# A two-layer diffusion trunk on one core: experts taken chunk by chunk in pairs, the small work in steps, and modulation by row sums

## The chip, the cores and the metric

The kernel runs on one core of one Trainium2 chip. The metric is the device time of one execution in microseconds (us); the time before is the median of three runs. Five engines work side by side, each through its own instructions in a fixed order: TensorE (PE in the profile, its weight loads PEld), VectorE (DVE), ScalarE (ACT), GpSimd (POOL) and SyncE (SP), which here issues the DMAs. What an engine waits for are semaphores of the others.

## The reference, cut to what matters

Layer 0 is a bidirectional gated linear recurrence with a dense SwiGLU; layer 1 is windowed attention with a mixture of experts. Every sub-layer is modulated (shift, scale, gate) from a conditioning vector for the 256 latent tokens and from another for the 256 context tokens. Only latent tokens come out of layer 1.

```python
D_MODEL, SEQ, CTX_LEN, D_FF = 1024, 256, 256, 2816
N_EXPERTS, TOP_K, D_EXPERT = 8, 2, 3584
# modulation of a layer: silu(c) @ w_mod + b_mod  -> 6 parts of 1024 (shift, scale, gate, twice)
def moe_swiglu(h, router, w_gate_up, w_down):        # h: 256 latent tokens
    logits = h @ router
    gates = softmax of each token's two largest logits, zero for the other six experts
    for e in range(N_EXPERTS):
        g, u = split(h @ w_gate_up[e], 2)            # (1024, 7168)
        out += gates[:, e:e+1] * ((silu(g) * u) @ w_down[e])   # (3584, 1024)
```

## The kernel before, in words

All products run in fp32r. For accuracy each operand is split into a high part, the value rounded to fp32r by ScalarE (`hi = ACT copy`), and a low part, the rest (`lo = VectorE subtract`). `weights` loads 1 MB (128 x 2048 values) into a `raw` buffer by one DMA of SP's queue, makes `whi` on ScalarE and `wlo` on VectorE (`split_into`, lines 113 and 114). `mm3` is the product of two split operands in three matmuls: hi*hi, lo*hi, hi*lo (lines 129 to 131).

**Experts.** A kernel-made ranking puts the experts in the order 0 to 7 so that those with an even number ("heavy") have up to 128 tokens and those with an odd number ("light") up to 64. `gather` picks an expert's tokens with a one-hot matrix on TensorE (line 1196), applies shift and scale on ScalarE (1199) and splits the outcome (1202, 1203). A heavy expert's tokens are two stationary tiles (hi, lo) and take three matmuls a weight block; a light one's hi and lo stand side by side in the 128 columns of one tile, take two (1219, 1220), and the two halves are added by a matmul with `fold` (1262).

An expert has seven pieces of 512 hidden features. A piece needs six weights of 1 MB: four for gate and up (`moegu`, 48 matmuls of 512 columns when heavy, 32 when light) and two for down (`moed`, 24 or 16). `up` does the first four; the Silu and the product (1240 and 1242 for heavy, 1265 and 1269 for light) follow; `turned` transposes a heavy piece (1249), and `down` of a piece comes after `up` of the next one. When an expert ends, `finished` multiplies by the gate row and splits (1289), and `scatter` puts the rows back (1301 to 1303).

The loop `run` takes the experts one after another, 0 to 7: seven heavy pieces, seven light pieces, and so on. The small work of a stage (`later`) is emitted all at once at the next opportunity; the gather for experts 2 and 3 is emitted in one go after a weight of a light piece.

**Order.** A scheduler emits each engine's instructions by priority; `after(n)` hangs an instruction behind the split of the n-th weight that is prepared and not yet taken by TensorE. `take` keeps three weights prepared ahead. There are four `whi`, four `wlo` and, in this stage, nine `raw` buffers (four, four in the pool `late`, one in the place of `x`), so the DMA queue can run nine weights ahead of VectorE.

**PSUM.** The eight banks are four of tag `a` (gate and up, gather, scatter), two of `b` (down), two of `c` (transposes, fold).

**Modulation.** Two forms exist. `modulation` loads two 1 MB weights and multiplies on TensorE with 32-column stationary tiles (line 176), copies, transposes back (184) and reduces: it does all of layer 0 and chunks 10 and 11 of layer 1. Layer 0's chunks 10 and 11 are done between the two halves of the recurrence's out-projection, layer 1's two inside the attention loop (units 0 and 6). `modulation1` instead takes a transposed 1 MB weight and lets VectorE multiply each row with the conditioning row and sum it (line 221, four instructions a weight, two blocks of rows by two conditioning vectors): 20 such weights, one behind each hidden block of the dense SwiGLU.

Of the kernel before, what the change touches and what calls it, by code (L numbers as in the profile page):

```python
# [45 lines left out]
PE_MOD1 = (10, 11)  # L46
DVE_MOD1 = tuple(c for c in range(24) if c // 2 not in PE_MOD1)

# [6 lines left out]
class Trunk:  # L55
# [113 lines left out]
    def modulation(self, layer, cc, tag="a"):  # L169
# [3 lines left out]
        for kh in range(2):  # L173
            w = self.raw(self.ins["wmod0"][cc - 1, kh] if layer == 0 else self.ins["wmod1"][PE_MOD1.index(cc), kh], 2048).rearrange("p (k n) -> p k n", k=4)
            for j in range(4):
                nc.tensor.matmul(part[32 * j:32 * j + 32, :], self.cs[:, kh * 4 + j, :], w[:, j, :],
                                 start=(kh == 0), stop=(kh == 1), tile_position=(0, 32 * j))
# [3 lines left out]
        def finish():  # L181
# [3 lines left out]
            m = self.mod[layer][:, cc * 4:cc * 4 + 4, :]  # L185
            nc.vector.tensor_reduce(m, tr.rearrange("p (f j m) -> p f m j", f=4, j=4)[:, :, 0:2, :], axis=AX.X, op=ALU.add)
            self.modbias(layer, cc * 4, 4)
# [21 lines left out]
    def modbias(self, layer, f, n):  # L209
        m = self.mod[layer][:, f:f + n, :]  # L210
        b = self.bmod[:, layer, f:f + n].unsqueeze(2).to_broadcast([P, n, 2])
        self.nc.vector.tensor_tensor(m, m, b, op=ALU.add)

    def modulation1(self, n):

        nc = self.nc
        c = DVE_MOD1[n]
        w = self.raw(self.ins["wmod1t"][n], 2048).rearrange("p (b k) -> p b k", b=2)
        for b in range(2):
            for who in range(2):  # L220
                nc.vector.scalar_tensor_tensor(self.junk, w[:, b], 1.0, self.crow[:, who], op0=ALU.mult, op1=ALU.mult,  # L221
                                               accum_out=self.mod[1][:, 2 * c + b, who:who + 1])
        self.modbias(1, 2 * c, 2)
# [70 lines left out]
    def hgrn2(self):  # L294
        nc, ins = self.nc, self.ins
        with ExitStack() as es:
# [18 lines left out]
            def begin():  # L315

                with ExitStack() as es_st:
# [61 lines left out]
                    for d in range(KB):  # L379
                        now = [[t[:, at] for t in w] for at in cols(d)]  # L380
                        more = d == 0 or d % 2 == 1 and d < KB - 1
                        if more:
                            finish = self.modulation_block(1, "c") if d == 0 else self.modulation(0, (d + 1) // 2, "c")
# [190 lines left out]
            for hd in range(HEADS):  # L574
# [10 lines left out]
                if hd == HEADS - 1:  # L585
                    for i in range(HEADS - 2):
                        turn(i)
                    done += [self.modulation(0, c) for c in (8, 9)]
# [3 lines left out]
                done = [self.modulation(0, c) for c in {2: (4,), 4: (5,), 5: (6,), 6: (7,)}.get(hd, ())]  # L592
# [35 lines left out]
    def dense(self):  # L628
        nc, ins = self.nc, self.ins
        with ExitStack() as es:  # L630
            h = self.h
            for s in self.outproj(ins["hgout"], 0, (0, 1), [(d, 0) for d in range(4)] + [(0, 1)], HALF, self.squares):
                if s == 0:
                    late = [self.modulation(0, cc) for cc in (10, 11)]
                self.normalizer(s)
                self.modulated(0, 3, s)
            for f in late:
                f()
# [26 lines left out]

            def down(g, acts):
                for c in range(4):
                    w = [t.rearrange("p (k n) -> p k n", k=KB) for t in self.weights(ins["ffd"][g, c], 2048)]
# [48 lines left out]
            for f in range(2, FB):  # L717
# [3 lines left out]
                if f < 2 + len(DVE_MOD1):  # L721
                    self.modulation1(f - 2)
# [27 lines left out]
    def attention(self):  # L750
        nc, ins = self.nc, self.ins
        with ExitStack() as es:
# [162 lines left out]
            for n in range(len(units) + 3):  # L915
                if n in (4, 8):
                    normq(n // 4 + 1, queries(n // 4 + 1))
                if n in (0, 6):
                    finish = self.modulation(1, PE_MOD1[n // 6], "b")
# [4 lines left out]
                if n in (1, 7):  # L924
                    finish()
# [26 lines left out]
    def experts(self):  # L952
        nc, tc, ins = self.nc, self.tc, self.ins
        with ExitStack() as es:
# [12 lines left out]
            self.slots["raw"] += [(self.pool(es, "late"), 4), (None, 1)]  # L967
# [102 lines left out]
            def spare():  # L1070
                at = D + next(turns) % 2 * NT
                return rest[:, at:at + NT]

            def weigh():
# [4 lines left out]
                few, wide = spare(), spare()  # L1079
# [82 lines left out]
            ex = self.pool(es, "ex")  # L1162

# [10 lines left out]
            def gather(ks, over):  # L1174
# [3 lines left out]
                for k in ks:  # L1178
                    onehot(k, over, slice(at, at + P))
                    light = k % 2 == 1 and not over  # L1180
                    m = LIGHT if light else P
                    xe[k] = slice(at, at + m), self.h[k // 2 % 2][:, :, P:2 * P] if light else [t[:, :, k % 2 * P:k % 2 * P + P] for t in self.h]
                    at += P
# [6 lines left out]
                terms = [(src[:, i], hot[:, i, :width]) for src in (th, tl) for i in range(2)]  # L1190
                for c in range(4):
# [5 lines left out]
                    u = spare()[:, :2 * width].rearrange("p (k n) -> p k n", k=2)  # L1197
                    for q in range(2):
                        nc.scalar.activation(u[:, q], g[:, q], AF.Identity, scale=self.mcol(1, 4, 2 * c + q, 0), bias=self.mcol(1, 3, 2 * c + q, 0))
                    for cols, x in xe.values():  # L1200
                        hi, lo = [t[:, two] for t in x] if isinstance(x, list) else (x[:, two, :LIGHT], x[:, two, LIGHT:])
                        nc.scalar.activation(hi, u[:, :, cols], AF.Copy)
                        self.gathered = nc.vector.tensor_tensor(lo, u[:, :, cols], hi.bitcast(F32), op=ALU.subtract).ins
                out = {}
                for n, (k, (_, x)) in enumerate(xe.items()):
# [3 lines left out]
                    hotT = ex.tile([P, 2 * P], F32R, name="hotT", tag="hotT", bufs=3)  # L1209
                    nc.scalar.activation(hotT, tp[:, :2 * P], AF.Copy)  # L1210
                    out[k] = x, hotT
                return out
# [11 lines left out]
            def up(xe, ahead, later):  # L1224
                gu = [self.bank("a") for _ in range(2)]
                light = not isinstance(xe, list)
                out = [spare() for _ in range(1 + light)]
                for j in range(2):
                    for kh in range(2):
# [4 lines left out]
                        while later:  # L1234
                            later.pop(0)()
                    if light:
# [70 lines left out]
            def run(over, ready, early=()):  # L1307
# [47 lines left out]
                while later:  # L1355
                    later.pop(0)()
# [110 lines left out]
```

## Time and profile before

| | |
|---|---|
| median of three runs | 1922.15 us (1921.99 to 1923.66) |
| profiled execution | 1922.4 us, of which the span from first to last instruction is 1920.2 us |
| PE, PEld, DVE, ACT, POOL busy | 1840.5, 1515.9, 1517.8, 1098.6, 174.1 us |
| experts, from the first weight split to the end | about 967 to 1920 us of the span |
| read from HBM | 477.1 MB, 249 GB/s over the span |

A row of the profile names the source line, the engine, the operation and the tiles (out<-in). Matmuls overlap: the time from one start to the next, not the duration shown, is what a matmul costs in a full queue; the same holds to a smaller degree on VectorE.

### The profile page before, as it was taken

How to read it: one execution, taken by the hardware profiler on the slowest of the kernel's cores; microseconds unless marked ns; L12 is line 12 of the kernel's file. 1: busy time of each engine (PE TensorE's matmuls, PEld its weight loads, DVE VectorE, ACT ScalarE, POOL GpSimd, SP SyncE). 2: the span in 40 equal slices, each digit the busy share in tenths (PEclk: the TensorE clock that was granted, in tenths of full speed). 3: DMA queues.
4: the chain of work that ended last, by engine and by line, in shares of the span. 5: the costliest groups of instructions: out<-in, count | busy, mean ns of one | idle time of the engine just before them, and what ended most of it. 6: DMA issues, size and time to landing. Idle time of an engine off the chain costs nothing.

```text
span 1920.2 us, 29477 instructions
## 1 busy us (share of the span) xinstructions
PE 1840.5 (96%) x11516; PEld 1515.9 (79%) x11516; DVE 1517.8 (79%) x2033; ACT 1098.6 (57%) x1311; POOL 174.1 (9%) x168
## 2 busy tenths in 40 slices
PE   7999999999999999989999999999999999999997
PEld 5888887898888888877887877787687877878775
DVE  5787778578566664768488799988998889898897
ACT  3433333443222223457676789777886778867785
POOL 2243233100000000323300000000000000000000
PEclk8999999999999999999999999999999999999998
DMA  7312333366444442032569899999999999999994
GB/s 280 143 63 74 122 119 126 139 241 219 147 161 155 159 152 83 16 132 107 224 238 371 320 402 397 359 370 384 384 389 349 369 381 390 390 334 380 381 393 158
DMA packets 73810, 480.13 MB, mean 250 GB/s; under 512 B 8768, under 2 KB 11456, under 8 KB 18752
## 3 DMA queue, kind: packets, MB, share of 16 engines
q1 hardware_dynamic: 73664, 478.18, 65.5%
q8 instruction: 92, 1.51, 0.3%
q14 instruction: 54, 0.44, 0.1%
HBM read 477.10 MB, written 1.05 MB: 249 GB/s over the span
## 4 chain that ended last, share of the span: by engine, by line
PE 30%; DVE 13%; issue 6%; ACT 5%; DMA 0%; POOL 0%; DVEq 0%; ACTq 0%; POOLq 0%
DVE wlo L114 9%; PE ps_a L130 5%; PE ps_a L131 5%; PE ps_a L129 5%; ACT whi L113 4%; PE ps_b L129 2%; PE ps_b L130 2%; PE ps_b L131 2%; PE ps_a L1220 1%; PE ps_a L1219 1%; PE ps_b L1220 1%; PE ps_c L1262 1%; PE ps_b L1219 1%; PE ps_a L1196 1%; DVE acc L1303 1%
## 5 line engine op out<-in xcount | busy, mean ns | idle before, releaser
L114 DVE TENSOR_TENSOR wlo<-raw,whi 128x2048 fp32r<-128x2048 f32 (+2 forms) x382 | 798.6, 2118 | 63.7 <-ACT whi L113 63.4
L113 ACT ACTIVATE whi<-raw 128x2048 fp32r<-128x2048 f32 (+2 forms) x418 | 685.6, 1676 | 263.1 <-PE ps_a L130 207.9
L130 PE MATMUL ps_a<-hlo,whi 128*128 128x512 f32 (+1 forms) x800 | 283.4, 355 | 3.2 <-DVE hlo L286 3.0
L129 PE MATMUL ps_a<-hhi,whi 128*128 128x512 f32 (+1 forms) x800 | 283.2, 358 | 1.5 <-ACT hhi L113 0.7
L131 PE MATMUL ps_a<-hhi,wlo 128*128 128x512 f32 (+1 forms) x800 | 282.8, 354 | 0.2 <-POOL wlo L114 0.2
L130 PE MATMUL ps_a<-wlo,hhi 128*128 128x512 f32 (+1 forms) x720 | 257.2, 357 | 8.3 <-DVE wlo L114 8.3
L129 PE MATMUL ps_a<-whi,hhi 128*128 128x512 f32 (+1 forms) x720 | 258.5, 359 | 2.2 <-ACT hhi L361 2.0
L131 PE MATMUL ps_a<-whi,hlo 128*128 128x512 f32 (+1 forms) x720 | 255.5, 356 | 2.4 <-DVE hlo L363 2.4
L130 PEld LDWEIGHTS ps_a<-hlo,whi 128*128 128x128 f32 x800 | 152.4, 191 | 23.4 <-DVE hlo L286 4.0
L129 PEld LDWEIGHTS ps_a<-hhi,whi 128*128 128x128 f32 x800 | 151.5, 190 | 23.8 <-ACT hhi L113 1.1
L131 PEld LDWEIGHTS ps_a<-hhi,wlo 128*128 128x128 f32 x800 | 152.2, 191 | 20.4 <-POOL wlo L114 0.4
L130 PEld LDWEIGHTS ps_a<-wlo,hhi 128*128 128x128 f32 x720 | 138.2, 192 | 29.7 <-DVE wlo L114 11.0
L129 PEld LDWEIGHTS ps_a<-whi,hhi 128*128 128x128 f32 x720 | 138.4, 192 | 26.3 <-issue 2.8
L131 PEld LDWEIGHTS ps_a<-whi,hlo 128*128 128x128 f32 x720 | 138.0, 192 | 21.3 <-DVE hlo L363 2.9
L221 DVE SCALAR_TENSOR_TENSOR junk<-raw,crow 128x1024 f32<-128x1024 f32 x80 | 97.8, 1222 | 33.3 <-DMA raw<-wmod1t 32.0
L1220 PE MATMUL ps_a<-wlo,hlo 128*128 128x512 f32 x224 | 91.8, 411 | 10.2 <-DVE wlo L114 9.1
L1220 PE MATMUL ps_a<-wlo,hhi 128*128 128x512 f32 x224 | 91.7, 411 | 7.4 <-DVE wlo L114 6.7
L1219 PE MATMUL ps_a<-whi,hhi 128*128 128x512 f32 x224 | 90.7, 408 | 0.0
L1219 PE MATMUL ps_a<-whi,hlo 128*128 128x512 f32 x224 | 89.8, 404 | 0.0
L1220 PE MATMUL ps_b<-wlo,eahi 128*128 128x512 f32 x224 | 86.6, 416 | 3.1 <-DVE wlo L114 2.4
L114 DVE TENSOR_TENSOR wlo<-x,whi 128x2048 fp32r<-128x2048 f32 x37 | 84.6, 2287 | 4.1 <-ACT whi L113 4.1
L130 PE MATMUL ps_b<-wlo,eahi 128*128 128x512 f32 x224 | 87.8, 392 | 0.0
(382 smaller groups left out, 3067.5 us busy)
## 6 DMA issues: line engine op xcount, KB each, us to landing
raw<-moegu SPq DMA_DIRECT2D x185, 1024.0 KB, 7.4
raw<-moed SPq DMA_DIRECT2D x108, 1024.0 KB, 7.3
x<-moegu SPq DMA_DIRECT2D x37, 1024.0 KB, 7.6
raw<-wmod SPq DMA_DIRECT2D x26, 1024.0 KB, 5.5
raw<-ffgu SPq DMA_DIRECT2D x22, 1024.0 KB, 4.8
raw<-wmod1t SPq DMA_DIRECT2D x20, 1024.0 KB, 4.9
raw<-whead SPq DMA_DIRECT2D x14, 768.0 KB, 4.5
raw<-ffd SPq DMA_DIRECT2D x8, 1024.0 KB, 4.8
```

Of the source, the lines that this page charges most:

```text
L113: high = self.nc.scalar.activation(hi[:, at], x[:, at], AF.Copy)
L114: low = (by or self.nc.vector).tensor_tensor(lo[:, at], x[:, at], hi[:, at].bitcast(F32), op=ALU.subtract)
L129: mm(out, l[0], r[0], start=first, stop=False)
L130: mm(out, l[0], r[1], start=False, stop=False)
L131: mm(out, l[1], r[0], start=False, stop=last)
L221: nc.vector.scalar_tensor_tensor(self.junk, w[:, b], 1.0, self.crow[:, who], op0=ALU.mult, op1=ALU.mult, accum_out=self.mod[1][:, 2 * c + ...
L1196: nc.tensor.matmul(g[:, q], l[:, 2 * c + q], r, start=(n == 0), stop=(n == 3))
L1219: nc.tensor.matmul(out, l, r[0], start=first, stop=False)
L1220: nc.tensor.matmul(out, l, r[1], start=False, stop=last)
L1262: nc.tensor.matmul(to[:, f], x[:, f * P:(f + 1) * P], fold, start=True, stop=True)
L1303: nc.vector.scalar_tensor_tensor(acc[:, i, cols], o, gate[:, i, e:e + 1], acc[:, i, cols], op0=ALU.mult, op1=ALU.add)
```

## The change

Four edits go together.

1. **Pieces take turns.** `run` orders the work as two heavy pieces, then a heavy and a light piece by turns (heavy piece n beside light piece n-2), and at the end two light pieces. An expert pair (0 and 1, 2 and 3, ...) is therefore in work at the same time, so `b` has four banks, `a` three and `c` one.
2. **Small work in steps.** `gather`, `turned`, `folded` and `finish` become generators; `tick` runs one step of each after every weight, and each step's ScalarE and VectorE instructions are hung behind the split of a weight one to three ahead.
3. **Buffers.** The room for three scratch rows (`room`) and the light experts' tokens (`xl`) comes from the pool `late`: two `raw` buffers there in place of four, seven in all.
4. **Modulation.** Layer 0's chunks 10 and 11 (as blocks 20 to 23) and layer 1's chunks 10 and 11 go to VectorE's row sums, 28 weights in place of 20; layer 1's from block 8 on are summed for the latent vector alone. There are 80 row-sum instructions before and after. Eight of the 28 stand in the dense SwiGLU's two `down` calls.

```diff
-DVE_MOD1 = tuple(c for c in range(24) if c // 2 not in PE_MOD1)
+DVE_MOD = [(0, c, 2) for c in range(20, 24)] + [(1, c, 2 if c < 8 else 1) for c in range(24)]
...
-                if s == 0:
-                    late = [self.modulation(0, cc) for cc in (10, 11)]
...
             def down(g, acts):
                 for c in range(4):
+                    self.modulation_rows(next(rows))
...
-                if f < 2 + len(DVE_MOD1):
-                    self.modulation1(f - 2)
+                self.modulation_rows(next(rows))
...
-                if n in (0, 6):
-                    finish = self.modulation(1, PE_MOD1[n // 6], "b")
...
-            self.slots["raw"] += [(self.pool(es, "late"), 4), (None, 1)]
+            self.slots["raw"] += [(self.pool(es, "late"), 2), (None, 1)]
...
+            self.banks(a=3, b=4, c=1)
+            later = []
+            def tick():
+                for task in later[:]:
+                    if next(task, later) is later:
+                        later.remove(task)
...
                 for j in range(2):
                     for kh in range(2):
                         w = [t.rearrange("p (k n) -> p k n", k=4) for t in self.take(ahead)]
...
+                        if kh and light:
+                            with self.after(2):
+                                nc.scalar.copy(both[j], gu[j])
+                        elif kh and not j:
+                            later.append(turned(gu, act))
+                        tick()
...
+            def turned(gu, act):
+                yield
+                sg = spare(3)
+                with self.after(2):
+                    nc.scalar.activation(sg, gu[0], AF.Silu)
+                yield
+                yield
+                with self.after(1, True):
+                    self.mark = nc.vector.tensor_tensor(sg, gu[1], sg, op=ALU.mult).ins
+                yield
...
+                    heavy, light = ([(e, c) for e in range(i, NE, 2) for c in range(EC)] for i in range(2))
+                    work = heavy[:2]
+                    for n in range(2, len(heavy)):
+                        work += [heavy[n], light[n - 2]]
+                    work += light[-2:]
```

Two places in the built program show the move. The first is VectorE's order where a heavy expert ends (before: the first light piece has begun; the names: `x<-ps_b` is `finished`, `x<-ps_c` and `eahi<-x` the product and low part of a light piece).

```order
L114 TENSOR_TENSOR wlo<-raw,whi 128x2048 x5
L114 TENSOR_TENSOR wlo<-x,whi 128x2048
L1289 TENSOR_TENSOR x<-ps_b,x 128x512
L114 TENSOR_TENSOR wlo<-raw,whi 128x2048 x2
L1269 TENSOR_TENSOR x<-ps_c,x 128x256
L114 TENSOR_TENSOR wlo<-raw,whi 128x2048
L1273 TENSOR_TENSOR eahi<-x,eahi 128x4x64
L1289 TENSOR_TENSOR x<-ps_b,x 128x512
```

The same place of the changed kernel, where a light expert ends between two heavy pieces (`room<-ps_a` and `ealo<-ps_c` belong to a heavy piece, `room<-ps_b` is `finish`):

```order
L1270 TENSOR_TENSOR room<-ps_a,room 128x512
L113 TENSOR_TENSOR wlo<-raw,whi 128x2048 x2
L1322 TENSOR_TENSOR room<-ps_b,x 128x512 x2
L113 TENSOR_TENSOR wlo<-raw,whi 128x2048
L1282 TENSOR_TENSOR ealo<-ps_c,eahi 128x512
L113 TENSOR_TENSOR wlo<-raw,whi 128x2048
L1331 TENSOR_TENSOR ealo<-room,eahi 128x512 x2
L113 TENSOR_TENSOR wlo<-raw,whi 128x2048 x2
L1341 SCALAR_TENSOR_TENSOR acc<-ps_a,gate,acc 128x512
```

The multiplications by the gate row now stand together, and heavy and light steps lie between the same weight splits.

The second is ScalarE's order in the gather for a heavy and a light expert together (`mod_96` is the scale and shift; 192 columns are 128 heavy and 64 light tokens). Before:

```order
L1199 ACTIVATE x<-ps_a,mod_96 128x192 x2
L1202 ACTIVATE hhi<-x 128x2x128
L1202 ACTIVATE hhi<-x 128x2x64
L113 ACTIVATE whi<-raw 128x2048
L1199 ACTIVATE x<-ps_a,mod_96 128x192 x3
```

Changed:

```order
L1210 ACTIVATE room<-ps_a,mod_96 128x192 x2
L112 ACTIVATE whi<-raw 128x2048
L1214 ACTIVATE hhi<-room 128x2x128
L1214 ACTIVATE xl<-room 128x2x64
L1210 ACTIVATE room<-ps_a,mod_96 128x192 x2
L112 ACTIVATE whi<-raw 128x2048
L1214 ACTIVATE hhi<-room 128x2x128
L1214 ACTIVATE xl<-room 128x2x64
```

A weight split now lies in every step of the gather, and on TensorE eight weight matmuls or more lie between two of its steps.

More of the change, by code (lines that the diff above doesn't have):

```diff
@@ L167, in setup, with modulation @@
         self.mod = [c.tile([P, 48, 2], F32, name=f"mod{i}") for i in range(2)]
-    def modulation(self, layer, cc, tag="a"):
+    def modulation(self, cc, tag="a"):
         nc = self.nc
@@ L1172, in onehot, with gather @@
                 self.routed = made.ins
-            def gather(ks, over):
+            def gather(ks, over, ready):
                 at, xe = 0, {}
[L1178 to L1183, printed above, removed]
+                with self.after(1, True):
+                    for k in ks:
+                        onehot(k, over, slice(at, at + P))
+                        light = k % 2 == 1 and not over
+                        m, n = LIGHT if light else P, (k % 2 if over else k // 2 % 2) * P
+                        xe[k] = slice(at, at + m), xl[:, :, n:n + P] if light else [t[:, :, n:n + P] for t in self.h]
+                        at += P
                 if ks[0] == 0 and not over:
@@ L1222, in experts, with up @@
             block = lambda x, f: [t[:, f] for t in x] if isinstance(x, (list, tuple)) else x[:, f]
-            def up(xe, ahead, later):
+            def up(xe, ahead):
                 gu = [self.bank("a") for _ in range(2)]
                 light = not isinstance(xe, list)
-                out = [spare() for _ in range(1 + light)]
+                both, act = [spare(next(turns) % 3) for _ in range(2 * light)], []
                 for j in range(2):
@@ L1305, in scatter @@
                             nc.sync.dma_start(self.out[0, i * P:(i + 1) * P, cols], acc[:, i, cols])
-            def run(over, ready, early=()):
-                work = [(e, c) for e in range(NE) for c in range(EC)]
-                left, y, due, later = None, None, None, []
-                self.take, self.after = feed(work, early)
-                def finish(k, hotT, y):
-                    nonlocal due
-                    due = k, hotT, finished(y)
-                def prepare(*ks):
-                    ready.update(gather(ks, over))
+                        yield
@@ new lines, in run @@
+            def run(over, early=()):
+                if over:
+                    work = [(e, c) for e in range(NE) for c in range(EC)]
+                else:
+                    heavy, light = ([(e, c) for e in range(i, NE, 2) for c in range(EC)] for i in range(2))
[3 more added lines that the diff above has]
+                    work += light[-2:]
+                left, ready, at, ys = None, {}, {}, {}
+                self.take, self.after = feed(work, early)
+                later.append(gather((0,), over, ready))
+                drain()
@@ L1321, in run @@
                 for e, c in work + [(NE, 0)]:
[L1322 to L1323 removed]
                     if e < NE:
[L1325 to L1330 removed]
+                        if c == 0:
+                            at[e] = ready.pop(e)
@@ L1331, in run @@
+                        act = up(at[e][0], 0 if (e, c) == (0, 0) and early else 3)
+                    if e == NE or not left:
+                        drain()
                     if (e, c) == (0, 0) and not over:
```

208 lines of the change are left out of this document (103 added, 105 removed).

## Prediction

> **What bounds the kernel now.** I read the page's slices first, then busy times by stage, then VectorE's and TensorE's timelines inside one piece of each kind.
>
> ```profile
> PE   7999999999999999989999999999999999999997
> DVE  5787778578566664768488799988998889898897
> PEclk8999999999999999999999999999999999999998
> DMA  7312333366444442032569899999999999999994
> ...
> 430.00:710.00 280.00, 280.00 (x1293) 234.13 (x1292) 191.97 (x276) 70.81 (x62) 0.00 (x0) 1.00 0.47 166
> 1200.00:1321.00 121.00, 118.78 (x535) 97.05 (x535) 107.72 (x66) 85.62 (x61) 0.00 (x0) 1.00 0.97 366
> 1321.00:1437.00 116.00, 108.42 (x515) 85.99 (x514) 108.78 (x77) 98.27 (x92) 0.00 (x0) 0.97 0.99 388
> 1370.00:1415.00 45.00, 41.79 (x202) 33.66 (x201) 41.86 (x32) 39.29 (x46) 0.00 (x0) 0.92 1.01 423
> ```
>
> Each column is a slice of 48 us; the experts fill the right half. In the stretch rows the columns are TensorE, its weight loads, VectorE, ScalarE, GpSimd, granted clock, DMA share, GB/s. The dense layer (430 to 710) is TensorE alone. A heavy expert (1200 to 1321) is nearly so; in a light one (1321 to 1437) VectorE is as busy and TensorE idles and once loses its clock. No resource is far from full over the whole half, so the question is what each needs for a pair of pieces, and the timelines tell:
>
> ```profile
> 1245.24 2.29 DVE L114 TENSOR_TENSOR wlo<-raw,whi 128x2048 fp32r<-128x2048 f32 x1 [0.91 <-ACT whi L113]
> 1248.24 0.69 DVE L1242 TENSOR_TENSOR x<-ps_a,x 128x512 f32<-128x512 f32 x1 [0.71 <-PE ps_a L131]
> 1248.85 4.49 DVE L114 TENSOR_TENSOR wlo<-raw,whi 128x2048 fp32r<-128x2048 f32 x2
> 1253.85 4.48 DVE L114 TENSOR_TENSOR wlo<-raw,whi 128x2048 fp32r<-128x2048 f32 x2
> 1262.05 2.29 DVE L114 TENSOR_TENSOR wlo<-raw,whi 128x2048 fp32r<-128x2048 f32 x1 [1.51 <-ACT whi L113]
> 1265.06 0.69 DVE L1242 TENSOR_TENSOR x<-ps_a,x 128x512 f32<-128x512 f32 x1 [0.71 <-PE ps_a L131]
> ...
> 1374.77 0.42 DVE L1269 TENSOR_TENSOR x<-ps_c,x 128x256 f32<-128x256 f32 x1
> 1375.11 2.29 DVE L114 TENSOR_TENSOR wlo<-raw,whi 128x2048 fp32r<-128x2048 f32 x1
> 1389.06 0.42 DVE L1269 TENSOR_TENSOR x<-ps_c,x 128x256 f32<-128x256 f32 x1
> ...
> 1237.07 0.39 PE L129 MATMUL ps_a<-whi,hhi 128*128 128x512 f32 x1
> 1237.30 0.40 PE L130 MATMUL ps_a<-wlo,hhi 128*128 128x512 f32 x1
> 1384.11 1.00 PE L1262 MATMUL ps_c<-fold,x 128*128 128x64 f32 x8
> 1384.91 0.48 PE L1219 MATMUL ps_a<-whi,hlo 128*128 128x512 f32 x1
> ```
>
> A heavy piece recurs after 1265.06 - 1248.24 = 16.8 us, a light one after 1389.06 - 1374.77 = 14.3. A 512-column matmul starts every 0.23 us (0.227 when 48 are averaged), a low split every 4.48 - 2.29 = 2.2, an operation on 512 columns takes 0.6 (1248.24 to 1248.85), on 256 columns 0.34 (1374.77 to 1375.11). So a heavy piece is 72 x 0.227 + transposes 0.4 = 16.8 us of TensorE, gapless, with VectorE idle 2.2 of them (1.51 + 0.71). A light one is 48 x 0.227 + two fold groups of 0.8 = 12.5 us of TensorE but 6 x 2.2 + 2 x 0.34 = 13.9 of VectorE, and takes 14.3. The two kinds are bound by different engines, and each wastes the other's time.
>
> **Sum for an expert pair.** The same wait recurs where a light expert has begun:
>
> ```profile
> 1337.03 0.69 DVE L1289 TENSOR_TENSOR x<-ps_b,x 128x512 f32<-128x512 f32 x1 [2.67 <-PE ps_c L1262]
> 1572.50 0.69 DVE L1289 TENSOR_TENSOR x<-ps_b,x 128x512 f32<-128x512 f32 x1 [2.67 <-PE ps_c L1262]
> ...
> L1303 DVE SCALAR_TENSOR_TENSOR acc<-ps_a,gate,acc x32: 742/748/751, 1120.1 to 1912.7; 128x512 f32<-128x512 f32 x32
> ...
> 1168.55 0.39 PE L1196 MATMUL ps_a<-hot,hlo 128*128 128x192 f32 x2
> 1168.78 0.39 PE L1196 MATMUL ps_a<-hot,hhi 128*128 128x192 f32 x2
> ```
>
> Two experts take 235.5 us. By pieces that is 7 x (16.8 + 14.3) = 217.7; the other 17.8 are gather, scatter and the change of kind. Interleaved, each resource needs:
>
> - TensorE: 7 x (16.8 + 12.5) = 205.1, scatter 16 x 0.23 = 3.7, gather 32 matmuls, two in 0.23 us = 3.7, token transposes 0.5: 213.
> - VectorE: 84 x 2.2 = 184.8; heavy 7 x 2 x 0.6, light 7 x 2 x 0.34 = 13.2; two endings of 4 x 0.6 + 4 x 0.66 = 10; gather 3: 211.
> - DMA: 84 MB-loads of 1.049 MB = 88.1 MB at 423 GB/s = 208.
>
> TensorE stays last. The most that interleaving can give is 4 x (235.5 - 213) = 90 us.
>
> **What of it is lost.** A pair of pieces is 29.3 us on TensorE, 28.3 on VectorE, 12.58 MB / 423 = 29.7 on the DMA queue. Bounds for its true length: 29.3 (nobody waits) and 31.1 (nothing is evened out, 16.8 + 14.3). The weights' four `whi` slots even out little: over the six light weights TensorE needs 10.9 us and VectorE 13.2, a lag of 2.3, about the one split that stands ready. Each small step is hung behind the split of a weight one to three ahead; if its input is late, the next split queues behind it and TensorE waits for that weight. I take 0.4 over TensorE's 29.3, the DMA row being the nearest: 26 pairs, 10 us (ends 0 and 47).
>
> Gather: ScalarE does two activations, 0.50 each, and two copies of 0.41 and 0.30 in each step beside a 1.9 us split, 3.6 us against TensorE's 1.8 + 0.9. Four such steps put it up to 3.6 us behind; before, the same waits cost TensorE its clock:
>
> ```profile
> 1404.00:1408.00 4.00, 1.91 (x9) 1.91 (x10) 3.85 (x6) 3.15 (x6) 0.00 (x0) 0.73 1.01 420
> 1408.00:1413.00 5.00, 5.00 (x14) 3.89 (x14) 3.62 (x7) 4.41 (x8) 0.00 (x0) 0.53 1.02 423
> ...
> L1199 ACT ACTIVATE x<-ps_a,mod x40: 386/496/517, 961.7 to 1648.9; 128x192 f32<-128x192 f32 x24, 128x128 f32<-128x128 f32 x8, 128x64 f32<-128x64 f32 x8
> ...
>   PE ps_a L1196: 6.3, 3
> ...
> L1202 ACT ACTIVATE hhi<-x x24: 296/412/429, 962.5 to 1649.6; 128x256 fp32r<-128x256 f32 x16, 128x128 fp32r<-128x128 f32 x8
> ...
> L113 ACT ACTIVATE whi<-raw 128x2048 fp32r<-128x2048 f32 x291 | 545.4, 1911 | 30.9 <-PE ps_a L131 13.8 <-PE ps_b L131 7.0 <-issue 6.3
> ```
>
> TensorE waits 6.3 us for the activations in three waits and then runs at half clock (0.53). With eight weight matmuls between steps no such idle stretch is left. I take 2.5 us a gather, four of them: 10 (ends 0 and 14).
>
> Endings: 5 us of VectorE work each, of which 1 us a pair of pieces is covered by its slack; 0.75 each remains, eight: 6 (ends 0 and 40). The two light pieces left alone at the end stay at 14.3: 2 x 1.8 = 3.6. The start keeps its form: ranking, first gather and VectorE's waits there,
>
> ```profile
> 1021.63 6.70 DVE L114 TENSOR_TENSOR wlo<-raw,whi 128x2048 fp32r<-128x2048 f32 x3 [2.07 <-ACT whi L113]
> 1030.95 2.29 DVE L114 TENSOR_TENSOR wlo<-x,whi 128x2048 fp32r<-128x2048 f32 x1 [2.63 <-ACT whi L113]
> ```
>
> of which I leave 8 of the 90 (these two are 4.7; ends 0 and 12). Sum: 90 - 10 - 10 - 6 - 4 - 8 = 52.
>
> **Buffers.** Nine raw buffers become seven.
>
> ```profile
> raw<-moegu SPq DMA_DIRECT2D x185, 1024.0 KB, 7.4
> ```
>
> A load lands 7.4 us after its issue, three splits of 2.45; two buffers more are in ScalarE's and VectorE's hands. Five of seven would do. Cost 0, and its cover, the two left over, is 4.9 us; were it gone, see the first rival.
>
> The Trainium skill (DMA: Bandwidth & Descriptors, "Where 436 GB/s comes from") says that loads from HBM are bound by about 358 GB/s a core. By that a pair would take 35.1 us, more than 31.1, and the change would lose; the row above has 423 GB/s over 45 us, and the measurement decides.
>
> **Modulation.** Off the old paths come TensorE's chunks in the out-projection and in attention; to the dense layer goes VectorE work.
>
> ```profile
> L176 PE MATMUL ps_a<-raw,cs x32: 592/592/617, 394.6 to 397.7; 128*32 128x512 f32 x32
> L176 PE MATMUL ps_b<-raw,cs x32: 592/592/617, 831.3 to 869.0; 128*32 128x512 f32 x32
> ...
> L221 DVE SCALAR_TENSOR_TENSOR junk<-raw,crow x80: 1214/1224/1228, 429.3 to 704.9; 128x1024 f32<-128x1024 f32 x80
>   DMA raw<-wmod1t: 32.0, 10
> ...
> L291 DVE SCALAR_TENSOR_TENSOR x<-ps_a,mod,x x72: 473/483/491, 382.3 to 952.2; 128x256 f32<-128x256 f32 x72
> ```
>
> Two chunks hold TensorE from 394.6 to 397.7 and the last 0.6, about 3.6 us between the out-projection's halves; attention's two have the same 32 instructions, worth the same if TensorE sets the pace there and nothing if not. Ends 0 and 7, taken 5. In the dense layer the count of row sums is the same, 80; eight weights move into `down` steps, where VectorE then has 4 x 1.3 + 2.2 + 4 x 0.5 = 9.4 us under 48 x 0.227 = 10.9 of TensorE. The row sums wait for their own loads (32 us in ten waits), with the next weight's split queued behind them; TensorE was busy 280.00 of 280 in spite of it, and DMA runs at 166 GB/s there, so I cost it at 0 (to +8 if a `down` step loses its 1.5 us of cover).
>
> **Total.** The profiled execution took 1922.4 us (span 1920.2 and 2.2 around it; the median of the runs is 1922.15). 1922.4 - 52 - 5 = 1865.
>
> **Rivals.**
> - *The DMA queue becomes the bound* (slower). With two buffers fewer the rate falls to that of the heavy expert, 366 GB/s: a pair takes 34.4 us, 26 x 3.3 = +86, less some 25 for gathers, endings and modulation: 1983. It ends slower from about 393 GB/s down, where a pair's 32.0 us (12.58 MB) are 0.9 above the 31.1 now and eat the 25. Against it: 366 is just what a heavy piece asks for (6.29 MB / 16.8 = 375). The Trainium skill's rule above points this way.
> - *Turns do not even out* (the change does not do what it says): four `whi` slots are too few, ScalarE's copies of the small work stand behind a split each, and a pair stays near 31. Then only gathers, endings and modulation gain, 25 to 30: 1895.
> - *Nobody waits*: every pair 29.3, gathers and endings free: 90 - 4 - 8, and 7 for modulation: 1837.
>
> **Chances.** Forecast, 1850 to 1880: 0.56. Nobody waits: 0.14. No evening out, 1880 to 1915: 0.2. DMA bound: 0.05. The rest, about 1922, 0.05. So faster 0.93, same 0.02, slower 0.05; 0.2% is about what a measurement of this kernel can tell from no change. The range, 1838 to 1898, leaves out the DMA bound and the edges of two rivals.
>
> **What would show it.** Right: pieces of alternating kind with 29.3 to 30 us from one heavy product (line 1270) to the next; expert pairs of 216 to 222 us; DMA at 400 GB/s or more throughout; no half-clock stretch at a gather; TensorE still gapless in the dense layer, no line-176 rows there after 390 us. Wrong: VectorE or ScalarE waiting more than 1.5 us a pair (four slots), TensorE waiting for a bank `a` (three in place of four) whose copy stands behind a 1.9 us split, DMA at 370 with empty raw buffers, or a `down` step of the dense layer over 10.9 us.

## The result, and the profile after

The changed kernel takes 1861.25 us (1861.09 to 1863.59, four runs) against 1922.23 (1921.99 to 1923.66): a ratio of 0.9689, with a 95% interval of 0.967 to 0.9708. It is 61 us faster. The profiled execution took 1861.09 us, its span is 1859.3.

The slices of its page, 46 us each:

```profile
PE   8999999999999999998899999999999999999996
DVE  5787778679876453776748999999999999999997
PEclk8999999999999999999999999999999999999998
DMA  7412323426556452111338999999999999999994
```

TensorE, VectorE and the transfers are now all three at nine tenths or more through the experts; before, VectorE's digit went to and fro between 8 and 9. Stretches of the same kernel (columns as before: TensorE, weight loads, VectorE, ScalarE, GpSimd, clock, DMA share, GB/s):

```profile
430.00:710.00 280.00, 280.00 (x1280) 233.54 (x1279) 190.94 (x280) 71.43 (x63) 0.00 (x0) 1.00 0.55 199
1160.90:1378.80 217.90, 216.44 (x1033) 179.28 (x1033) 212.15 (x141) 182.62 (x149) 0.00 (x0) 1.00 1.00 405
1378.80:1596.80 218.00, 216.55 (x1034) 179.43 (x1033) 212.25 (x142) 182.72 (x149) 0.00 (x0) 1.00 1.00 405
1596.80:1809.10 212.30, 211.98 (x997) 175.42 (x997) 208.95 (x129) 176.78 (x131) 0.00 (x0) 1.00 1.01 412
```

The first is the dense layer, still gapless with the row sums in it. The others are three turns of two experts, bounded by the ending of a heavy one (line 1322); the clock stays at 1.00 in all three. VectorE's timeline shows the pairs of pieces inside the middle one (line 1297 is a light piece's product, once a pair):

```profile
1160.86 0.68 DVE L1322 TENSOR_TENSOR room<-ps_b,x 128x512 f32<-128x512 f32 x1
...
1378.82 0.68 DVE L1322 TENSOR_TENSOR room<-ps_b,x 128x512 f32<-128x512 f32 x1
...
1411.81 0.42 DVE L1297 TENSOR_TENSOR x<-ps_c,x 128x256 f32<-128x256 f32 x1
1440.10 0.42 DVE L1297 TENSOR_TENSOR room<-ps_c,room 128x256 f32<-128x256 f32 x1
1473.16 0.42 DVE L1297 TENSOR_TENSOR x<-ps_c,x 128x256 f32<-128x256 f32 x1
1502.76 0.42 DVE L1297 TENSOR_TENSOR x<-ps_c,x 128x256 f32<-128x256 f32 x1
1537.96 0.43 DVE L1297 TENSOR_TENSOR room<-ps_c,room 128x256 f32<-128x256 f32 x1 [0.45 <-ACT room L1294]
...
1596.76 0.68 DVE L1322 TENSOR_TENSOR room<-ps_b,x 128x512 f32<-128x512 f32 x1
```

Two experts take 218 us in place of 235.5. From one light product to the next the seven pairs take 33.3 (with an ending), 28.3, 33.1 (with the other ending), 29.6, 35.2 (with the gather), 28.8 and 29.7. The mark is an operation of VectorE, and a neighbour's weight split can fall on either side of it, so sums over several pairs say more than one pair.

Of TensorE's waits the one that shrank most is that for a light weight's low half. From the waits between 965 and 1860 us (what waited, for what: us in total, times, longest), first of the kernel before, then of the one after:

```profile
PEld ps_a L1220 <- DVE wlo L114: 36.9, 52, 1.9
```

```profile
PEld ps_a L1236 <- DVE wlo L113: 6.3, 16, 0.5
```

Ahead of the experts almost nothing is left of the gain. The last matmuls of the out-projection, the last mix of values in attention, and the first logit, before and after:

```profile
L130 PE MATMUL ps_a<-hlo,ohi x64: 280/283/283, 383.2 to 418.8; 128*128 128x256 f32 x64
...
L905 PE MATMUL ps_c<-pt,V x256: 272/273/477, 848.5 to 924.8; 128*64 128x128 f32 x128
...
L1039 DVE SCALAR_TENSOR_TENSOR logit<-ps_c,rstd,base x2: 216/220/225, 956.6 to 956.8; 128x8 f32<-128x8 f32 x2
```

```profile
L129 PE MATMUL ps_a<-hlo,ohi x64: 281/283/283, 383.3 to 415.4; 128*128 128x256 f32 x64
...
L902 PE MATMUL ps_c<-pt,V x256: 272/273/476, 840.3 to 925.0; 128*64 128x128 f32 x128
...
L1032 DVE SCALAR_TENSOR_TENSOR logit<-ps_c,rstd,base x2: 216/220/225, 955.6 to 955.8; 128x8 f32<-128x8 f32 x2
```

The out-projection ends 3.4 us earlier; attention ends where it did. From the logit to the end it is 1920.2 - 956.6 = 963.6 us before and 1859.3 - 955.6 = 903.7 after: 59.9 of the 61 us come from the experts.

### The profile page after: what moved, and what is told of

It is laid out like the page before. It is cut to its first block, busy times and chain, and to the rows that moved or that the text cites. A ratio compares the mean times of both kernels' runs of the same rounds, so it can differ in the third digit from the quotient of the medians.

```text
span 1859.3 us, 29342 instructions
## 1 busy us (share of the span) xinstructions
PE 1800.8 (97%) x11436; PEld 1504.2 (81%) x11436; DVE 1518.0 (82%) x2033; ACT 1101.6 (59%) x1307; POOL 175.2 (9%) x168
## 4 chain that ended last, share of the span: by engine, by line
PE 78%; DVE 11%; ACT 5%; issue 3%; DMA 1%; POOL 1%; SPq 0%; DVEq 0%; ACTq 0%; POOLq 0%
PE ps_a L128 16%; PE ps_a L129 16%; PE ps_a L130 16%; PE ps_a L1236 4%; DVE wlo L113 4%; PE ps_a L1235 4%; PE ps_b L129 3%; ACT whi L112 2%; PE ps_b L130 2%; PE ps_b L128 2%; PE ps_c L1291 2%; PE ps_b L1235 2%; PE ps_b L1236 2%; PE ps_b L461 1%; PE ps_c L538 1%
## 5 line engine op out<-in xcount | busy, mean ns | idle before, releaser
L112 ACT ACTIVATE whi<-raw 128x2048 fp32r<-128x2048 f32 (+2 forms) x404 | 670.1, 1681 | 290.5 <-PE ps_a L129 210.8
L113 DVE TENSOR_TENSOR wlo<-raw,whi 128x2048 fp32r<-128x2048 f32 (+2 forms) x368 | 772.7, 2127 | 39.0 <-ACT whi L112 38.1
L129 PE MATMUL ps_a<-wlo,hhi 128*128 128x512 f32 (+1 forms) x720 | 253.2, 352 | 0.8 <-DVE wlo L113 0.8
L1235 PE MATMUL ps_a<-whi,xl 128*128 128x512 f32 x448 | 178.7, 399 | 4.0 <-DVE acc L1341 3.7
L1236 PE MATMUL ps_a<-wlo,xl 128*128 128x512 f32 x448 | 177.9, 397 | 0.6
L113 DVE TENSOR_TENSOR wlo<-x,whi 128x2048 fp32r<-128x2048 f32 (+1 forms) x51 | 109.9, 2160 | 3.7 <-ACT whi L112 3.7
L1236 PEld LDWEIGHTS ps_a<-wlo,xl 128*128 128x128 f32 x448 | 84.8, 189 | 22.9 <-DVE wlo L113 6.3
L1235 PEld LDWEIGHTS ps_a<-whi,xl 128*128 128x128 f32 x448 | 84.8, 189 | 22.1 <-issue 5.6
L112 ACT ACTIVATE whi<-x 128x2048 fp32r<-128x2048 f32 (+1 forms) x51 | 92.3, 1815 | 15.7 <-PE ps_a L130 6.9
L129 PE MATMUL ps_b<-wlo,eahi 128*128 128x512 f32 x224 | 90.5, 404 | 2.3 <-DVE wlo L113 2.3
```

The costliest lines, as they stand in the source:

```text
L112: high = self.nc.scalar.activation(hi[:, at], x[:, at], AF.Copy)
L113: low = (by or self.nc.vector).tensor_tensor(lo[:, at], x[:, at], hi[:, at].bitcast(F32), op=ALU.subtract)
L129: mm(out, l[0], r[1], start=False, stop=False)
L1235: nc.tensor.matmul(out, l, r[0], start=first, stop=False)
L1236: nc.tensor.matmul(out, l, r[1], start=False, stop=last)
```

## The experiments

Twelve kernels in three sets, each set on one chip; the kernel before ran beside each set (1920.0, 1922.05 and 1922.5 us), so ratios to it are compared across sets.

**Modulation alone, and all but modulation.** One kernel is the old experts with the new rest, the other the new experts with the old rest. The edit between old and new rest, in short (the chunks' data and the other calls go with it):

```diff
-                if n in (0, 6):
-                    finish = self.modulation(1, PE_MOD1[n // 6], "b")
...
-                if f < 2 + len(DVE_MOD1):
-                    self.modulation1(f - 2)
+                self.modulation_rows(next(rows))
```

> The kernel before with the change's new modulation alone (twelve TensorE chunks become row sums in the dense layer and leave the out-projection and attention); experts untouched. The prediction's term is 5 us: 1917. Theory (gained and given back): the out-projection gains 3.4 us, attention, where the removed matmuls stood in idle time, gives most of it back: 1920 to 1922. Rival (a saving that stays): 1916 to 1918.

> The kernel after with the old modulation: TensorE's chunks stand again in the out-projection and in attention, the experts as changed. Theory (gained and given back): 1861 to 1863, nothing or 1 us above the changed kernel. Rival (a saving that stays): 1865 to 1867.

Measured: 1918.86 us (1908.52 to 1921.44), ratio 0.9993 (0.9982 to 1.0005), and 1863.96 us, ratio 0.9704 (0.969 to 0.9717), where the whole change has 0.9689 (0.967 to 0.9708) and its repeat below 0.97. Both medians lie between theory and rival. The new modulation is worth some 1 us by itself and 0 to 5 beside the new experts: the intervals hold no change, and do not exclude the 5. The traces above are sharper: gained and given back. It is the modulation's doing and not the new experts': the mix of values in attention runs from 841.4 to 924.6 us with the new modulation and the old experts, and from 850.1 to 926.5 with the old modulation and the new experts (before 848.5 to 924.8, after 840.3 to 925.0, above).

**Attention: who gave it back.** When the queries are normalized for the third time, the kernel after is still 4.3 us ahead (883.07 against 887.34 us); 40 us later it is not. With the modulation's weights gone from the stream, the raw buffers that they held let the out-projection's loads start earlier. From SP's timeline, before, then after:

```profile
868.79 21.32 SPq L105 DMA_DIRECT2D raw<-swout  x4
```

```profile
843.97 42.22 SPq L104 DMA_DIRECT2D raw<-swout  x4
```

So ScalarE splits five quarter weights in a row at 886.7 us, and GpSimd makes six low halves without a pause, in a stretch in which VectorE is the pace of attention. GpSimd before, then GpSimd and VectorE in the kernel after:

```profile
892.31 2.68 POOL L114 TENSOR_TENSOR wlo<-raw,whi 128x512 fp32r<-128x512 f32 x2 [4.91 <-ACT whi L113]
```

```profile
887.43 7.64 POOL L113 TENSOR_TENSOR wlo<-raw,whi 128x512 fp32r<-128x512 f32 x6 [4.02 <-ACT whi L112]
...
883.88 0.17 DVE L273 SCALAR_TENSOR_TENSOR rq<-rq 128x8 f32<-128x8 f32 x1
888.96 1.23 DVE L273 SCALAR_TENSOR_TENSOR rq<-rq 128x8 f32<-128x8 f32 x1
890.11 0.68 DVE L867 TENSOR_REDUCE st<-ps_a 128x1 f32<-128x512 f32 x1
893.86 1.23 DVE L870 TENSOR_TENSOR st<-st,rq 128x2 f32<-128x2 f32 x1
```

The same operation on 8 columns takes 0.17 us ahead of GpSimd's stretch and 1.23 in it, 1.06 us longer, where a low half takes 1.27; the reduction from PSUM keeps its 0.68. ScalarE then waits 2.95 us for VectorE (`st`, L871) and TensorE 3.18 for ScalarE, and a half-clock stretch of 6.8 us follows (granted clock 0.71 from 890 to 900, 1.00 in the kernel before). Three edits were run beside a repeat of the kernel after. `att_spread` hangs each quarter split of the out-projection behind a copy of turned scores:

```diff
+            self.held = self.pts[15:32]      # one copy of turned scores each
-            high = self.nc.scalar.activation(hi[:, at], x[:, at], AF.Copy)
+            with self.tc.issue_after(self.held.pop(0)) if self.held else nullcontext():
+                high = self.nc.scalar.activation(hi[:, at], x[:, at], AF.Copy)
```

`att_fill` puts unread products where the modulation's had been, and `att_both` does both:

```diff
+                if n in (0, 6):
+                    self.keep_warm(self.bank("b"), self.x[:, 1, 0], 4)
```

> The kernel after, unchanged, beside the next three on their chip: 1859 to 1863 by every theory; it is the base that they are measured against.

> The kernel after, but ScalarE's splits of the out-projection's first weights in attention are held so that at most one quarter weight is split behind each copy of turned scores, where the kernel after has five in a row at 884 to 888 us and GpSimd then six low halves in a row (887.4 to 895.1). Theory (GpSimd's low halves, which the freed raw buffers let come earlier and closer together, slow VectorE's small operations in the stretch where VectorE sets attention's pace, and so give back 4 of the 5 us that the modulation gained): VectorE's operations there return to 0.16 us and attention ends 3 to 4 us earlier, 1857 to 1858. Rival (the TensorE clock, or attention's own VectorE work, sets the end): no change, within 1.5 us of the base.

> The kernel after, with four matrix products whose result nobody reads (128x128 by 256 columns each, some 1.8 us together) put on TensorE at attention's units 0 and 6, where the kernel before had the modulation's matmuls. Theory (the removed matmuls had kept TensorE's clock up; without them a half-clock stretch of 6.8 us at 832 appeared): that stretch goes, and 2 to 4 us with it: 1857 to 1859. Rival (GpSimd's low halves against VectorE): no gain, 1861 to 1864.

> The kernel after with both edits of attention: ScalarE's quarter splits held to one a copy, and the four unread products at units 0 and 6. Theory (both edits gained by the same thing, that the run of five splits was broken up; the products did nothing for the clock): no better than either alone, 1857 to 1860. Rival (two separate causes, which add: 3.7 us and 5.6 us of attention): 1853 to 1855.

Measured: 1864.18 us (1862.96 to 1865.82) for the repeat, 1859.69 (1857.31 to 1862.76), 1857.91 (1856.93 to 1858.59) and 1857.89 (1856.64 to 1860.5). GpSimd and VectorE in `att_spread`, at the same place:

```profile
887.68 1.33 POOL L115 TENSOR_TENSOR wlo<-raw,whi 128x512 fp32r<-128x512 f32 x1 [4.02 <-ACT whi L114]
891.35 1.26 POOL L115 TENSOR_TENSOR wlo<-raw,whi 128x512 fp32r<-128x512 f32 x1 [2.34 <-ACT whi L114]
896.87 1.27 POOL L115 TENSOR_TENSOR wlo<-raw,whi 128x512 fp32r<-128x512 f32 x1 [4.26 <-ACT whi L114]
...
889.21 0.15 DVE L275 SCALAR_TENSOR_TENSOR rq<-rq 128x8 f32<-128x8 f32 x1
```

The low halves stand apart, the same small operation is at 0.15 us again (another, on 2 columns, still takes 1.26 beside the low half at 891.35), TensorE waits 1.62 us in place of 3.17 and keeps its clock (1.00 from 890 to 900, 0.86 in the repeat). Attention's last values are mixed at 921.5 us, in the repeat at 925.2: 3.7 us, as the theory named, but 0.9 of them were there at 884 us already, ahead of GpSimd's run, so 2.8 arise in it and behind it. The edit also takes ScalarE's five splits apart; in the repeat's trace it is VectorE that ScalarE and TensorE wait for there, so that is the likelier cause, though no run separates the two. `att_fill` was meant to test the clock. Its trace speaks against that: a half-clock stretch of 6.8 us stays at 837.8 (835.8 in the repeat), and up to 867 us it is within 1 us of the repeat. But GpSimd's low halves come two, one and three at a time as in the kernel before, the run of six is gone, and most of the 5.6 us (919.6) are gained behind 867. So it fits GpSimd's part without having been built for it, and how much of its gain the products themselves have stays open. Both together end attention at 917.4, earlier than either; the theory's "no better" holds for the total alone. In the profiled execution of `att_both` (1860.5 us, the longest of its five) longer half-clock stretches behind attention take it back: 10.2 us from 954.6 (6.8 in `att_fill`) and 3.4 us at each of two gathers (none in `att_fill`). By their ratios of 0.9667 and 0.9673, `att_fill` and `att_both` are the fastest kernels here that leave no product out, `att_fill` 6 us under the repeat.

The repeat itself is 3 us above the first measurement of the same kernel. Its trace has half-clock stretches of 3.4 us at two of the gathers (1102 and 1539 us), where the first trace has none, and the pairs there take 30.4 and 30.0 us in place of 28.8.

**The old order, with steps.**

```diff
-                if over:
+                if True:
                     work = [(e, c) for e in range(NE) for c in range(EC)]
```

and in the second also

```diff
-                    u = spare(4 - c % len(ks))[:, :2 * width].rearrange("p (k n) -> p k n", k=2)
+                    u = spare(c % len(ks))[:, :2 * width].rearrange("p (k n) -> p k n", k=2)
```

> The kernel after with the pieces in the old order (all eight of an expert, then all of the next), gathers, endings and the work of a piece still in steps. Theory (the turns carry the gain): light pieces are back at VectorE's 14 us and four expert pairs lose about 4 x 14 to 18 us: 1910 to 1925. Rival (the steps carry it, since they take the small work out of TensorE's way): 1865 to 1885.

> The same as the run with the pieces in the old order, with the gather's scratch moved to two tiles that are free in that order (there, the scratch of a gather and of a heavy piece were the same tile, which adds waits of one for the other). Theory (steps alone are worth 38 us, turns 21): 1880 to 1884, as before. Rival (the shared scratch had cost time): 1870 to 1878.

In the first of the two a gather's scratch and a heavy piece's product share a tile and overwrite one another, so its values are not the reference's; the second moves the scratch. They took 1881.95 us (ratio 0.9801, 0.9786 to 0.9817) and 1879.43 (0.978, 0.9765 to 0.9795). The theory that the turns carry the gain fell: all but the turns gains 42.6 us (steps, the gathers' new place, buffers, PSUM banks and modulation together), and turns another 15.3 (1879.43 to 1864.18, on one chip). The move of the scratch gained 2.5 us, or 4 by the ratios, and 1879.43 lies between its theory and its rival. Stretches of the second kernel, a light expert and then a heavy one, and the timeline of VectorE:

```profile
1340.00:1420.00 80.00, 76.49 (x364) 60.31 (x364) 80.00 (x49) 68.02 (x56) 0.00 (x0) 1.00 1.01 410
1210.00:1330.00 120.00, 120.00 (x567) 99.95 (x566) 111.11 (x77) 93.94 (x79) 0.00 (x0) 1.00 0.97 384
```

```profile
1330.01 0.68 DVE L1322 TENSOR_TENSOR room<-ps_b,x 128x512 f32<-128x512 f32 x1
1390.69 0.43 DVE L1297 TENSOR_TENSOR x<-ps_c,x 128x256 f32<-128x256 f32 x1
1404.57 0.43 DVE L1297 TENSOR_TENSOR x<-ps_c,x 128x256 f32<-128x256 f32 x1
1552.21 0.68 DVE L1322 TENSOR_TENSOR room<-ps_b,x 128x512 f32<-128x512 f32 x1
```

In the light expert VectorE is busy 80.00 of 80 us, and a piece takes 13.9 (14.3 before); in the heavy one TensorE is busy 120.00 of 120. Each kind is at its own bound without turns, and a turn of two experts takes 222.2 us. The gathers also moved: before, they stood in light pieces, where VectorE has no time (1389.06, 1404.37 and 1423.94 on its timeline of before: 15.3 and 19.6 us for two pieces of 14.3); now they stand behind a heavy expert's fifth piece.

**Gathers in one go, endings in two goes**, both with turns:

```diff
-                        later.append(gather((e + 1,) if over else (e + 2, e + 3), over, ready))
+                        for _ in gather((e + 1,) if over else (e + 2, e + 3), over, ready):
+                            pass
```

```diff
             def finish(e, hotT, y):
...
-                with self.after(1, True):
-                    for n in range(2):
-                        nc.vector.tensor_tensor(yg[n], y[n], gf[:, n * NT:(n + 1) * NT], op=ALU.mult)
-                yield
...
+                for n in range(2):
+                    nc.vector.tensor_tensor(yg[n], y[n], gf[:, n * NT:(n + 1) * NT], op=ALU.mult)
+                    self.split_into(hi, lo, yg[n])
+                for _ in range(3):
+                    yield
...
-                        yield
-                        with self.after(1, True):
-                            nc.vector.scalar_tensor_tensor(acc[:, i, cols], o, gate[:, i, e:e + 1], acc[:, i, cols], op0=ALU.mult, op1=ALU.add)
+                        nc.vector.scalar_tensor_tensor(acc[:, i, cols], o, gate[:, i, e:e + 1], acc[:, i, cols], op0=ALU.mult, op1=ALU.add)
```

> The kernel after with the three gathers of two experts each run in one go, as before the change, where the change gives them a step a weight; everything else as changed. Theory (a gather in one go makes TensorE wait for its activations and drops the clock): half-clock stretches of 3 to 7 us at each gather come back, 3 x 3 to 6 us: 1869 to 1880. Rival (with pieces taking turns TensorE has work enough to cover a gather, or the queue behind catches up): 1860 to 1863.

> The kernel after with each expert's ending in two goes, as before the change (scaling and split at once, then all scatter products and accumulations of four tiles at once three weights later), where the kernel after has nine steps, each placed behind a weight's split. The prediction's term for endings was 1 us each, about 8 in all, of which 6 would stay. Theory (steps took VectorE's bursts out of the weights' way, and most of the 32 us that steps gained beside the three gathers' 10.5 come from here): 1873 to 1885. Rival (an ending is covered by a pair's slack of 1 us of VectorE and by the buffers): 1861 to 1867.

Measured: 1871.73 us, ratio 0.9749 (0.9735 to 0.9764), and 1878.1, ratio 0.9782 (0.9759 to 0.9804). Against the change's 0.9689 and 0.97 in two sets these are 9 to 12 us for three gathers and 16 to 18 for eight endings. The pair with the gather, and the clock at another:

```profile
1509.91 0.41 DVE L1297 TENSOR_TENSOR x<-ps_c,x 128x256 f32<-128x256 f32 x1
1548.56 0.42 DVE L1297 TENSOR_TENSOR room<-ps_c,room 128x256 f32<-128x256 f32 x1
```

```profile
1529.00:1534.00 5.00, 4.69 (x16) 3.48 (x17) 2.04 (x7) 4.21 (x11) 0.00 (x0) 0.66 0.98 406
```

It is 38.7 us against 35.2, here with a stretch of half clock. The other two gathers in one go have none and still take 38.5 and 37.8 us against 35.9 and 35.2: the total lies in the theory's range, but the clock that it named is the smaller part, and what makes up the rest was not isolated. Of the endings in two goes the waits between 1130 and 1830 us tell, where the kernel after had 6.3 us in 16:

```profile
PEld ps_a L1236 <- DVE wlo L113: 23.3, 30, 2.1
```

The next weight's low half stands behind an ending's burst on VectorE, and TensorE waits for it. So gathers and endings in steps hold 25 to 30 of the 43 us that all but the turns gained, if they are worth as much without turns, which was not run.

**Five raw buffers.**

```diff
-            self.slots["raw"] += [(self.pool(es, "late"), 2), (None, 1)]
+            self.slots["raw"] += [(None, 1)]
```

> The kernel after with five raw weight buffers in the experts instead of seven. The prediction held that five would do and costed the step from nine to seven at 0. Theory (a load lands in some 7.9 us, three splits of 2.4; two more buffers are in the hands of ScalarE and VectorE): 1861 to 1866. Rival (transfers need more of them in flight to reach 430 GB/s): a pair of pieces over 31 us, 1905 or more.

Measured: 1879.45 us, ratio 0.9789 (0.9762 to 0.9816). Neither theory: 17 to 19 us slower than with seven, by the ratios of two sets. Waits between 1130 and 1830 us, and a turn of two experts:

```profile
ACT whi L112 <- DMA raw<-moegu: 44.0, 69, 2.1
...
ACT whi L112 <- DMA x<-moegu: 13.4, 22, 2.0
...
ACT whi L112 <- DMA raw<-moed: 8.1, 14, 0.8
...
ACT whi L112 <- DMA x<-moed: 3.0, 5, 1.0
```

```profile
1388.60:1612.00 223.40, 218.47 (x1033) 180.55 (x1032) 213.53 (x141) 185.37 (x149) 0.00 (x0) 0.99 0.99 395
```

With seven, no wait for a transfer stands in the list of the same stretch; with five ScalarE waits 68.5 us in 110 places, plain pairs of this turn are at 29.7 to 30.8 us, and the rate falls to 395 GB/s.

**What bounds a pair next.**

```diff
-                    self.mm3(out, l, r, first, last)
+                    nc.tensor.matmul(out, l[0], r[0], start=first, stop=False)
+                    nc.tensor.matmul(out, l[0], r[1], start=False, stop=last)
```

> The kernel after with two products in place of three for each block of a heavy expert's pieces (the low half of the activations times the high half of the weights is left out), so that TensorE's work in a pair of pieces falls from 29.3 to about 23.9 us. It asks what bounds a pair next. The prediction's bounds were 28.3 us for VectorE and 29.7 for the transfers at 423 GB/s. Theory (VectorE is next): pairs of 28.3, 26 us less, 1836 to 1842, at 445 GB/s. Rival (the transfers bound at 423 to 432 GB/s): pairs of 29.1 to 29.7, 1858 to 1864, no gain.

Measured: 1849.24 us, ratio 0.9628 (0.9602 to 0.9654): half of what the theory expected. A turn of two experts, its four pairs around the two endings and its three with the gather, then the same four and three in the kernel after:

```profile
1373.10:1589.70 216.60, 196.25 (x865) 146.04 (x866) 211.33 (x141) 180.86 (x148) 0.00 (x0) 0.98 1.00 408
1372.80:1496.00 123.20, 110.72 (x481) 80.83 (x480) 123.20 (x82) 101.26 (x76) 0.00 (x0) 1.00 1.01 414
1496.00:1589.40 93.40, 85.54 (x385) 65.19 (x384) 88.13 (x62) 79.60 (x72) 0.00 (x0) 0.96 0.98 399
```

```profile
1378.50:1502.80 124.30, 123.98 (x580) 101.92 (x579) 123.45 (x82) 102.55 (x77) 0.00 (x0) 1.00 1.00 407
1502.80:1596.50 93.70, 92.57 (x455) 77.50 (x455) 88.80 (x62) 80.17 (x72) 0.00 (x0) 1.00 0.99 403
```

A turn takes 216.6 us, only 1.4 less, although TensorE has 7 x 24 x 0.227 = 38 us less to do in it. The four pairs around the endings are VectorE's: busy 123.20 of 123.20 us here, and 123.45 of 124.3 in the kernel after. The three with the gather keep their length for another reason. Neither engine is full there: TensorE waits 3.2 us for ScalarE's copy of the token transposes (`hotT`) and then has a half-clock stretch of 6.8 us, which the trace of the kernel after does not have. Whose those three pairs are in the kernel after, this run cannot tell. The third turn has no gather, and there it can: its last three pairs take 88.1 us in the kernel after with TensorE busy all of them, and 85.1 here with VectorE busy 84.95. So VectorE is next, as the theory says, but more than half of a turn was VectorE's already, which is why so little is gained.

## Why the prediction was right, point by point

The total was right, 1865 against 1861.25, and the engines even out as named, but the gain was shared out wrongly between turns and steps, and three steps failed (endings, the ground for the buffers, attention's end). That the total fits is in part luck.

- **The experts' sum, 90 - 38 = 52.** 59.9 measured, so 30 are lost of the 90. The pair of two experts came out at 218.0 and 217.9 us, inside the 216 to 222 that were to show it right, at 405 GB/s. Of the other signs, 29.3 to 30 us from one heavy product (line 1270) to the next held for two of the seven pairs of the middle turn (29.0 to 35.0). A sign of being wrong was met and meant nothing: ScalarE waits more than 1.5 us a pair (for folds alone, L1294, 38.9 us in 22 places between 1130 and 1830 us), but it is busy 183 of 218 us and not the bound.
- **Pairs, 0.4 each.** The four plain pairs above sum to 116.4 us, 29.1 in the mean: the taken 29.7 was the transfers' bound at 423 GB/s, and the transfers did not bind. The 10 us of this term were not lost.
- **Endings, 0.75 each.** This step failed. It let 5 us of VectorE's work be covered by 1 us of slack a pair. The pair with an ending takes 28.3 + 5.0 = 33.3 us: in it nothing was covered. Over the four pairs around a turn's two endings VectorE needs 4 x 28.3 + 10 = 123.2 us and TensorE 4 x 29.3 + 2 x 1.8 (scatter) = 120.8; they take 124.3. That is 3.5 us for two endings, some 14 for eight in place of 6. "TensorE stays last" is true of the sums over two experts (213 against 211) and not of every stretch: around the endings VectorE is last. The run with two products shows it: these four pairs keep their length, 123.2 us, with 21.8 us less for TensorE. Why nothing evens out beyond such a stretch was not tried by itself; the seven raw buffers and four split ones hold less than the twelve weights of a pair.
- **Gathers, 2.5 each.** The three pairs with the gather take 93.7 us, TensorE needs 3 x 29.3 + 4.2 (matmuls and token transposes) = 92.1: 1.6 a gather. With the endings' 3.5 that is the turn: 213 + 5.1 = 218.1. Without steps a gather costs some 3 to 4 more, with the clock down at one of three. The term was about right; the reason, ScalarE falling behind in the gather, is seen in the run with two products (3.2 us for `hotT`).
- **What turns bring.** The rival without evening out stood at 1895, so 30 us were ascribed to turns and 25 to 30 to gathers, endings and modulation. Measured: 15 and 43. Light pieces were taken to stay at 14.3 us without turns; in steps, plain pieces of the old order already run at 16.8 and 13.9. The two errors cancelled in the total, which is luck.
- **Buffers.** From nine to seven cost nothing that shows, as costed. Its ground, that five would do, was wrong: five cost 17 to 19 us. The step divided a landing time of 7.4 us (a median; 7.9 after) by a pair's 2.45 us a weight; ScalarE's 110 waits for a transfer, 2.1 us at most, show that this leaves too little. Which part of a buffer's time the step left out was not shown.
- **Modulation, 5.** The out-projection's 3.6 us came (3.4), and the dense layer stayed free. Attention's end (0 to 3.6 was allowed) failed: by the first logit 2.4 us of the 3.4 are lost again, and 1.0 is left. The step counted the removed matmuls alone and not the raw slots that they had held; freed slots moved the out-projection's loads 25 us ahead, and GpSimd's splits into VectorE's way. `att_spread` ends attention 3.7 us earlier, 2.8 of them in that stretch.
- **Rivals.** The transfers kept 405 to 412 GB/s over whole turns of two experts, so the slow rival (366) fell. That is above the about 358 GB/s a core of the Trainium skill (DMA: Bandwidth & Descriptors, "Where 436 GB/s comes from"), and the measurement decides; it was taken with one core at work, and no run here shows two cores loading at once. "Nobody waits" (1837) fell at the endings.

## What to carry to other kernels

Before two streams with different bounds are interleaved, put the small work between their pieces into steps and away from the piece whose engine is full: here that, with the new modulation and buffers, gave 43 of 58 us, and the turns 15. Where two engines are both near full, sum the larger need stretch by stretch, bursts included (here 123.2 for VectorE and 92.1 for TensorE, 215.3 in all; 218 was measured), not each engine's need over the whole (213). When an edit takes loads out of a stream, look at which later loads inherit their buffers, and whose work these then start.

## What the runs showed of the hardware

While GpSimd subtracted two SBUF tiles six times in a row (1.27 us each), VectorE operations of 2 to 8 columns with their operands in SBUF took 0.63 to 1.23 us in place of 0.15 to 0.17 (two on 2 columns in the same stretch, at 892.57 and 893.79 us, stayed at 0.15), and a reduction from PSUM did not change. The Trainium skill (SBUF — State Buffer, "Who interferes with whom") says that a VectorE instruction with two SBUF inputs contends with a GpSimd instruction that reads SBUF, and that the ports the two share are an exclusive lock. The trace agrees for those with two inputs; two multiplications of one tile by a constant (L840) rose too, from 0.16 to 0.70 and 0.63. The price here was up to 1.08 us for an instruction of 2 to 8 columns, so it adds up where VectorE has many short ones.

TensorE's busy time is no measure of its work: in the four pairs around the endings, at a granted clock of 1.00, it has 4 x 24 x 0.227 = 21.8 us less to do with two products, and its busy time fell from 123.98 to 110.72, by 13.3, with VectorE as the bound. A share of 97% of the span did not mean that a lighter TensorE would help by as much.
